# Two-layer decoder trunk: PSUM banks of the expert loop's side work from two pools, lo splits at the routing off GpSimd, and the second token norm split between ScalarE and VectorE

## Chip, cores and metric

The kernel runs on one core of a Trainium2 chip. The metric is the device time of one execution, the median of three runs. Below, PE is TensorE, DVE is VectorE, ACT is ScalarE, POOL is GpSimd and SP is SyncE, which issues the loads. PSUM is the memory that PE writes its sums to; a bank of it holds 128 x 512 floats.

## What is computed

A trunk of two layers over 256 tokens of width 1024, float32 throughout. The tokens are normed, and then each layer mixes tokens (three attention-like head groups from one input projection) and mixes channels: layer 0 with a dense SwiGLU, layer 1 with eight SwiGLU experts of which each token takes two.

```
x = layer_norm(x, ln_emb_g, ln_emb_b)
for l in range(DEPTH):
    mix = hybrid_mixer(x, w_in[l], ...)            # h = x @ w_in, three head groups, @ w_o
    x = layer_norm(DN_ALPHA * x + mix, ln1_g[l], ln1_b[l])
    f = swiglu(x, ...) if l % 2 == 0 else moe_swiglu(x, router, w_gate, w_up, w_down)
    x = layer_norm(DN_ALPHA * x + f, ln2_g[l], ln2_b[l])

def moe_swiglu(...):                               # D = 1024, 8 experts, inner width 3584
    logits = xt @ w_router
    top_v, top_i = lax.top_k(logits, 2)
    gates = sum(one_hot(top_i) * softmax(top_v))
    for e in range(8):
        y = y + gates[:, e:e+1] * swiglu(xt, w_gate[e], w_up[e], w_down[e])
```

## The kernel before

Every float32 operand of a product is split in two: a hi half, which is the value rounded for PE (`whi`, a cast on ACT, L151), and a lo half, what is left (`wlo`, a subtraction, L152, on DVE or, where a plan says so, on POOL). A product is then three matmuls: hi by hi, lo by hi, hi by lo (`mm3`, L161 to L163). Weights come in raw buffers by DMA; a raw buffer comes free when its lo half is done, and only then does SP load the next weights into it.

The order of the work on each engine is made by a scheduler from the order of the code, with ties written by hand: `after(i)` puts the next instructions behind instruction i, and `hold_splits(...)` is a plan for the next splits, each with what they stand behind and the engine of the lo half. `START` and `NEXT` are such plans for the first projection of layers 0 and 1 (True means POOL), and `R1`, `R2` say behind which split of the projection the two pieces of work on the second 128 tokens are recorded.

*Start.* The tokens come in two halves of 128. Each is normed (`stats`: mean and variance on DVE, the root on POOL; `norm`: L1247 and L1250, scalar_tensor_tensor on DVE, 512 columns at a time), transposed by PE (`pt`, L166) and split (`xhi`, `xlo`). Between them the input projection for the first half runs on PE (`pj`), over four weight splits of 832 columns and more.

*Routing.* After layer 1's norm DVE finds each token's two experts in small steps of 8 columns (L699 to L712), PE counts positions (`pc`), DVE compares them with a ramp (`pm`, L729, a 0/1 matrix per expert), and PE gathers the tokens of an expert by a matmul with it (`gx`, L741). ACT copies the hi halves (L751) and DVE the lo halves (L749) out of PSUM into `xg`. Meanwhile the first expert's weights are split; a plan in `gather` says how.

*Expert loop.* Eight experts of seven steps: gate and up sums (`eg`, two banks of the pool `wps`), SiLU on ACT (L919), a product on DVE (`hh`, L925), a transpose (`ht`) and the down sums (`y`, two banks of the pool `acc`). Each pool has four banks, given out in turn. From the second expert on each step has two forms, chosen at run time: heavy (three matmuls per product) if the expert has more than 64 tokens, light (two) if not. In this input experts 0, 3, 5 and 6 are heavy. Two experts make a pair. Side work of the pairs, called chores, is done one at a time at certain points of a step (`point`): the gather of the next pair (`gx`, then casts to `xg`), the transposed 0/1 matrices with the gates (`gsb`, L800 and L802, copied out by ACT at L805 and L806) and the scatter of an expert's result to its tokens (`sc`, L993 and L994, added to the sum on DVE, L999, `r`). A chore's bank comes free when its copy or addition is done, which `defer` puts four weight splits of 1024 columns later.

Of the kernel before, what the change touches and what calls it, by code (L numbers as in the profile page):

```python
# [10 lines left out]
F32 = mybir.dt.float32  # L11
F32R = mybir.dt.float32r
BF16 = mybir.dt.bfloat16
AF = mybir.ActivationFunctionType
ALU = mybir.AluOpType
# [3 lines left out]
P = 128  # L19
D = 1024  # L20
# [14 lines left out]
EARLY = 11  # L35
WT = (3, 4)
START = (False, True, False, True)
R1, R2 = (0, 1), (0, 5)
WF = 6
HBUF = 3  # L40
NEXT = (True, False, True, False)
R3 = (0, 7)
WS = (8,3)
FENT = ((0, None, 2), (1, None, SPL))
# [42 lines left out]
def trunk(ctx: ExitStack, tc: tile.TileContext, x, consts, mconsts, vecs, lnrows, w_in, w_uq, w_ukv, w_o,  # L87
          ffn_gu, ffn_dn, router, e_gate, e_up, e_down, out):
    nc = tc.nc
# [4 lines left out]
    acc = ctx.enter_context(tc.tile_pool(name="acc", bufs=4, space=PS))  # L94
    wps = ctx.enter_context(tc.tile_pool(name="wps", bufs=4, space=PS))

    def bank(pool, name):
        return pool.tile([P, 512], F32, tag="acc" if pool is acc else "wps", name=name)
# [37 lines left out]
    plan = []  # L136
    last = [None, None]

    def after(*ins):
        st = ExitStack()  # L140
        for i in ins:
            st.enter_context(tc.issue_after(i.ins))
        return st
# [2 lines left out]

    def split(src, n, lo_eng=None, to=None):
        hi, lo = to or [spl[0].tile([P, 1024], F32R, tag=t, name=t) for t in ("whi", "wlo")]
        ins, eng = plan.pop(0) if plan else ((), lo_eng)
        with after(*ins):  # L150
            last[0] = nc.scalar.copy(hi[:, :n], src)  # L151
            last[1] = (eng or nc.vector).tensor_tensor(lo[:, :n], src, hi.bitcast(F32)[:, :n], ALU.subtract)  # L152
        return hi, lo

    def hold_splits(*steps):
        plan.clear()
        for ins, eng, n in steps:
            plan.extend([(ins, eng)] * n)

    def mm3(o, ahi, alo, bhi, blo, start, stop):  # L160
        nc.tensor.matmul(o, ahi, bhi, start=start, stop=False)  # L161
# [475 lines left out]
    def moe(pool, raws2, raws3, r, gb, rw):  # L637
# [32 lines left out]
        for tt in range(2):  # L670
            x1 = ya[tt]
            pw, nm = ln_norm(*r[tt], gb, t0[:, tt], x1)
            lt = bank(acc, "lgp")
            for q in range(2):
# [5 lines left out]
                i1 = nc.scalar.copy(xt, pt)  # L680
# [44 lines left out]
        def gather(pr):  # L725
            pm = pool.tile([P, 2, 256], F32R, tag="pm", name="pm")
            for tt in range(2):
                for j in range(2):
                    ip = nc.vector.tensor_scalar(pm[:, tt, j * P:(j + 1) * P], iota, posm[:, tt, 2 * pr + j:2 * pr + j + 1],  # L729
                                            None, ALU.is_equal)  # L730
            if pr == 0:
                hold_splits(((), None, 2), ((pw,), nc.gpsimd, 2), ((i1, pw), nc.gpsimd, 1), ((i1, ip), None, 3))
            xgs = [pool.tile([P, KD, P, 2], F32R, tag="xg", name="xg", bufs=3) for j in range(2)]

            def half_part(k2, hl, n=0):
                src = (xth, xtl)[hl]
                b = bank(acc, "gx")
                for kk in range(2):
                    k = 2 * k2 + kk
                    for tt in range(2):  # L740
                        nc.tensor.matmul(b[:, kk * 256:(kk + 1) * 256], src[:, tt, k * P:(k + 1) * P], pm[:, tt, :],  # L741
                                         start=(kk == 0 and tt == 0), stop=(kk == 1 and tt == 1))

                def copies():
                    bv = b.rearrange("p (a b) -> p a b", b=256)
                    for j in range(2):
                        o = xgs[j][:, 2 * k2:2 * k2 + 2, :, hl]
                        if hl:
                            nc.vector.tensor_copy(o, bv[:, :, j * P:(j + 1) * P])  # L749
                        else:  # L750
                            nc.scalar.copy(o, bv[:, :, j * P:(j + 1) * P])  # L751

                defer(n, copies)

            def part(k2):
                for hl in range(2):
                    half_part(k2, hl)

            return pm, xgs, part, half_part
# [26 lines left out]
        def gather2(pr, pm):  # L786
            gs = pool.tile([P, 2], F32, tag="gs", name="gs")
            pT = pool.tile([P, 2, 2, P], F32R, tag="pTm", name="pTm")
            sc[pr] = [(gs[:, j:j + 1], pT[:, j]) for j in range(2)]

            for j in range(2):
                for tt in range(2):
                    nc.vector.tensor_scalar(pm[:, tt, j * P + 64:(j + 1) * P], iota[:, 64:P],
                                            posds[0][:, tt, 2 * pr + j:2 * pr + j + 1], None, ALU.is_equal)
            pmf = pm.bitcast(F32)

            def one(j):
                b = bank(acc, "gsb")
                for tt in range(2):
                    nc.tensor.matmul(b[:, 256:264], pmf[:, tt, j * P:(j + 1) * P], gates[:, tt, :], start=(tt == 0), stop=False)  # L800
                for tt in range(2):
                    nc.tensor.matmul(b[:, tt * P:(tt + 1) * P], pmf[:, tt, j * P:(j + 1) * P], ident, start=False, stop=(tt == 1))  # L802

                def copies():
                    nc.scalar.copy(gs[:, j:j + 1], b[:, 256 + 2 * pr + j:257 + 2 * pr + j])  # L805
                    nc.scalar.copy(pT[:, j, :, :], b[:, 0:256].rearrange("p (a b) -> p a b", b=P))  # L806

                defer(CHORE_N, copies)

            return one  # L810
# [9 lines left out]

        chores = []
        points = [0]

        def point():
            points[0] += 1
# [163 lines left out]
            nc.vector.scalar_tensor_tensor(y[1], yb[n], gs, y[0].bitcast(F32), ALU.mult, ALU.subtract)  # L989

        def scatter(n, tt, y, pT, last=False):
            b = bank(acc, "sc")
            nc.tensor.matmul(b, pT[:, tt, :], y[0], start=True, stop=False)  # L993
            nc.tensor.matmul(b, pT[:, tt, :], y[1], start=False, stop=True)  # L994
            if last:
                ln_sum(ya[tt], ya[tt], {n: b}, fsums[tt], 1.0, (n,))
            else:
                cs = slice(n * 512, (n + 1) * 512)
                defer(CHORE_N, lambda: nc.vector.tensor_tensor(ya[tt][:, cs], ya[tt][:, cs], b, ALU.add))  # L999
# [181 lines left out]
    with tc.tile_pool(name="spl", bufs=SPL, reuse_waits="tile") as spl[0], \  # L1181
# [35 lines left out]
        def start(mp):  # L1217
            z = mp.tile([P, 256], F32, tag="mk4", name="z")
            nc.gpsimd.memset(z, 0.0)
            keep_warm(bank(wps, "kw"), z, WS[0], z[:, 0:P])  # L1220
            xin = [cpool.tile([P, D], F32, tag="r", name="r", bufs=2) for _ in range(2)]
            load(xin[0], x[0:P, :])
            load(ident, mconsts[:, M_ID:M_ID + 128])
            t = gb_load(0)
            gb = [t[i // 2][:, (i % 2) * 512:(i % 2 + 1) * 512] for i in range(4)]
            load(xin[1], x[P:S, :])
            raw = win_a(0)
            load(vec, vecs)
            xhi, xlo = x3(F32R, "xhi"), x3(F32R, "xlo")
            xres = []  # L1230

            def stats(tt):
                st = small.tile([P, 2, 6], F32, tag="xst", name="xst", bufs=2)
                mv = small.tile([P, 4], F32, tag="xmv", name="xmv", bufs=2)
                for n in range(2):
                    nc.vector.bn_stats(st[:, n, :], xin[tt][:, n * 512:(n + 1) * 512])
                nc.vector.bn_aggr(mv[:, 0:2], st)
                nc.gpsimd.tensor_scalar_add(mv[:, 2:3], mv[:, 1:2], LN_EPS)
                rpow(mv[:, 3:4], mv[:, 2:3], 1)
                return mv  # L1240

            def norm(tt, mv):
                xr = pre.tile([P, D], F32, tag="xr%d" % tt, name="xr")
                xres.append(xr)
                for n in range(2):
                    cs = slice(n * 512, (n + 1) * 512)
                    nc.vector.scalar_tensor_tensor(xr[:, cs], xin[tt][:, cs], mv[:, 0:1], gb[n], ALU.subtract, ALU.mult)  # L1247
                for n in range(2):
                    cs = slice(n * 512, (n + 1) * 512)
                    i = nc.vector.scalar_tensor_tensor(xr[:, cs], xr[:, cs], mv[:, 3:4], gb[2 + n], ALU.mult, ALU.add)  # L1250
                return i

            def second(i):
                with after(last[1]):
                    norm(1, mv1)

            def third(i):
                with after(i):
                    pt = to_T(xres[1])
                split_T(pt, 1, xhi, xlo)  # L1260

            norm(0, stats(0))
            pts = to_T(xres[0])
            keep_warm(bank(wps, "kw"), z, WS[1], z[:, 0:P])
            mv1 = stats(1)
            split_T(pts, 0, xhi, xlo)
            rest = {R1: second, R2: third}
            hold_splits(*(((), nc.gpsimd if g else None, 1) for g in START))
            return raw, (xhi, xlo, xres), rest
# [141 lines left out]
```

## Time and profile before

| | |
|---|---|
| median of 3 runs | 1471.09 us (1469.09 to 1473.74) |
| the profiled execution | 1468.16 us |
| its span in the trace | 1466.0 us |
| around the span | 2.16 us |
| PE, DVE, ACT, POOL busy | 93%, 80%, 68%, 5% |
| mean granted PE clock | 0.987 of full |

The times of the profile are in microseconds from the span's start. The start lies at 0 to 31, the mixer and the dense channel mixer of layer 0 up to 338, the mixer of layer 1 up to 465, the routing at 465 to 488, the experts up to about 1450. Shares of busy time are means over these stages.

### The profile page before, as it was taken

The page shows a single profiled execution, that of the slowest core. Times are in us where ns is not written, and L with a number is a line of the kernel's source. Part 1 is how long each engine was busy: PE and PEld are TensorE (multiplying, and loading weights), DVE is VectorE, ACT ScalarE, POOL GpSimd, SP SyncE. Part 2 cuts the span into 40 slices and gives each one's busy share as a digit, 9 for nine tenths or more (in the row PEclk, how much of TensorE's full clock was granted, in tenths as well). Part 3 has the DMA queues.
Part 4 walks back from the last instruction along what each step waited for, and adds up shares of the span by engine and source line. Part 5 has one row for each costly group of instructions (what it writes and reads, how often), then busy time and mean ns, then how long its engine had stood idle before and what let it go on. Part 6 is the DMA issues. An engine that isn't in the chain of part 4 may idle for free. (4 is left out here: it accounts for less than half of the span.)

```text
span 1466.0 us, 18597 instructions
## 1 busy us (share of the span) xinstructions
PE 1359.3 (93%) x6927; PEld 1118.0 (76%) x6927; DVE 1176.5 (80%) x1256; ACT 997.0 (68%) x1073; POOL 78.4 (5%) x113
## 2 busy tenths in 40 slices
PE   7999999999999899988989999998999999999895
PEld 6987999998987688766666677866677787787663
DVE  6577655557677788899999987898998788788996
ACT  3564444444565677788978877787986777778794
POOL 3011000004102100000000000000000000000101
PEclk9999999999999999999999999999999999999998
DMA  6733555544534699999999998899998799899980
GB/s 264 276 135 115 189 186 186 188 157 153 194 116 201 231 339 356 375 365 349 420 406 369 419 382 323 325 367 348 407 419 342 295 357 357 311 358 389 357 363 30
DMA packets 63513, 429.46 MB, mean 293 GB/s; under 512 B 7058, under 2 KB 7570, under 8 KB 15268
## 3 DMA queue, kind: packets, MB, share of 16 engines
q1 hardware_dynamic: 63364, 427.81, 76.4%
q8 instruction: 81, 1.33, 0.4%
q14 instruction: 36, 0.29, 0.1%
q0 software_dynamic: 32, 0.03, 0.0%
HBM read 426.76 MB, written 1.05 MB: 292 GB/s over the span
## 5 line engine op out<-in xcount | busy, mean ns | idle before, releaser
L152 DVE TENSOR_TENSOR wlo<-raw,whi 128x2048 fp32r<-128x2048 f32 (+4 forms) x475 | 911.0, 1939 | 158.3 <-ACT whi L151 156.7
L151 ACT CAST whi<-raw 128x2048 fp32r<-128x2048 f32 (+4 forms) x482 | 771.0, 1619 | 250.5 <-PE gu L585 44.0
L898 PE MATMUL eg<-wlo,xg 128*128 128x512 f32 x448 | 185.6, 414 | 22.1 <-DVE wlo L152 19.0
L162 PE MATMUL eg<-wlo,xg 128*128 128x512 f32 x448 | 178.0, 397 | 0.8 <-DVE wlo L152 0.3
L161 PE MATMUL eg<-whi,xg 128*128 128x512 f32 x448 | 178.6, 399 | 0.0
L897 PE MATMUL eg<-whi,xg 128*128 128x512 f32 x448 | 178.4, 398 | 0.0
L163 PE MATMUL eg<-whi,xg 128*128 128x512 f32 x448 | 176.6, 394 | 0.0
L898 PEld LDWEIGHTS eg<-wlo,xg 128*128 128x128 f32 x448 | 84.4, 188 | 70.4 <-DVE wlo L152 54.9
L971 PE MATMUL y<-wlo,wk 128*128 128x512 f32 x224 | 94.2, 421 | 17.0 <-DVE wlo L152 15.8
L162 PEld LDWEIGHTS eg<-wlo,xg 128*128 128x128 f32 x448 | 86.9, 194 | 21.5 <-DVE wlo L152 5.4
L163 PEld LDWEIGHTS eg<-whi,xg 128*128 128x128 f32 x448 | 86.7, 194 | 17.3
L584 PE MATMUL gu<-xhi,whi 128*128 128x256 f32 x352 | 99.8, 283 | 0.1
L585 PE MATMUL gu<-xlo,whi 128*128 128x256 f32 x352 | 99.7, 283 | 0.2 <-DVE xlo L224 0.2
L161 PEld LDWEIGHTS eg<-whi,xg 128*128 128x128 f32 x448 | 86.9, 194 | 16.7
L586 PE MATMUL gu<-xhi,wlo 128*128 128x256 f32 x352 | 99.6, 283 | 0.0
L897 PEld LDWEIGHTS eg<-whi,xg 128*128 128x128 f32 x448 | 84.9, 189 | 15.0 <-ACT whi L151 0.5
L971 PE MATMUL y<-whi,wk 128*128 128x512 f32 x224 | 90.3, 403 | 3.6 <-DVE wk L945 1.5
L162 PE MATMUL y<-wlo,wk 128*128 128x512 f32 x224 | 88.0, 393 | 3.6 <-DVE wlo L152 3.4
L161 PE MATMUL y<-whi,wk 128*128 128x512 f32 x224 | 87.5, 392 | 0.4 <-ACT hh L919 0.4
L163 PE MATMUL y<-whi,wk 128*128 128x512 f32 x224 | 87.3, 390 | 0.0
L971 PEld LDWEIGHTS y<-wlo,wk 128*128 128x128 f32 x224 | 44.1, 197 | 42.7 <-DVE wlo L152 36.0
L584 PEld LDWEIGHTS gu<-xhi,whi 128*128 128x128 f32 x352 | 67.6, 192 | 0.7 <-DVE xlo L224 0.3
(313 smaller groups left out, 2111.8 us busy)
## 6 DMA issues: line engine op xcount, KB each, us to landing
raw<-in_e_gate SPq DMA_DIRECT2D x112, 1024.0 KB, 7.1
raw<-in_e_up SPq DMA_DIRECT2D x110, 1024.0 KB, 7.2
raw<-in_e_down SPq DMA_DIRECT2D x108, 1024.0 KB, 7.4
raw<-in_ffn_gu SPq DMA_DIRECT2D x22, 1024.0 KB, 4.8
raw<-in_ffn_dn SPq DMA_DIRECT2D x11, 1024.0 KB, 4.7
raw<-in_w_in SPq DMA_DIRECT2D x10, 960.0 KB, 4.7
raw<-in_w_o SPq DMA_DIRECT2D x8, 1024.0 KB, 6.7
gb<-in_lnrows SPq DMA_DIRECT2D x8, 512.0 KB, 5.3
```

Source lines behind the costliest of these rows:

```text
L151: last[0] = nc.scalar.copy(hi[:, :n], src)
L152: last[1] = (eng or nc.vector).tensor_tensor(lo[:, :n], src, hi.bitcast(F32)[:, :n], ALU.subtract)
L161: nc.tensor.matmul(o, ahi, bhi, start=start, stop=False)
L162: nc.tensor.matmul(o, ahi, blo, start=False, stop=False)
L163: return nc.tensor.matmul(o, alo, bhi, start=False, stop=stop)
L584: nc.tensor.matmul(o, hi[:, cs], xhi[:, k, :], start=(g == 0 and k == 0), stop=False)
L585: nc.tensor.matmul(o, hi[:, cs], xlo[:, k, :], start=False, stop=False)
L586: nc.tensor.matmul(o, lo[:, cs], xhi[:, k, :], start=False, stop=(g == 1 and k == 7))
L897: nc.tensor.matmul(bs[g], x2, sp[k // 4][0][:, cs], start=(k == 0), stop=False)
L898: nc.tensor.matmul(bs[g], x2, sp[k // 4][1][:, cs], start=False, stop=(k == 7))
L971: nc.tensor.matmul(yb[n], h2, sp[j // 2][i][:, j % 2 * D + n * 512:j % 2 * D + n * 512 + 512], start=(m == 0 and j == 0 and i == 0), stop= ...
```

## The change

It has four parts. The banks of chores come from a function that takes `acc` and `wps` by turns; the first pair's gather and the last scatters stay in `acc`. The plan at the routing gives all lo halves to DVE, and those of the third to fifth split stand behind the last `pm` (plans can hold an extra tie for the lo half). The second half of the tokens is normed by an activation on ACT (scale and bias from `stats`, the bias by one more POOL operation) and two tensor_tensor of 1024 columns on DVE, the second of them recorded later. And the first lo half of layer 1's projection goes from POOL to DVE.

```diff
-R1, R2 = (0, 1), (0, 5)
+R1, R2 = (0, 3), (0, 5)
-NEXT = (True, False, True, False)
+NEXT = (False, False, True, False)
...
-        ins, eng = plan.pop(0) if plan else ((), lo_eng)
+        ins, eng, late = plan.pop(0) if plan else ((), lo_eng, ())
         with after(*ins):
             last[0] = nc.scalar.copy(hi[:, :n], src)
+        with after(*ins, *late):
             last[1] = (eng or nc.vector).tensor_tensor(lo[:, :n], src, hi.bitcast(F32)[:, :n], ALU.subtract)
...
-                hold_splits(((), None, 2), ((pw,), nc.gpsimd, 2), ((i1, pw), nc.gpsimd, 1), ((i1, ip), None, 3))
+                hold_splits(((), None, 2), ((i1,), None, 3, ip), ((i1, ip), None, 3))
...
-                b = bank(acc, "gx")
+                b = bank(acc, "gx") if pr == 0 else step_bank("gx")
...
-                b = bank(acc, "gsb")
+                b = step_bank("gsb")
...
+        turns = [0]
+
+        def step_bank(name):
+            turns[0] += 1
+            return bank((acc, wps)[turns[0] % 2], name)
...
-            b = bank(acc, "sc")
+            b = bank(acc, "sc") if last else step_bank("sc")
...
             def second(i):
-                with after(last[1]):
-                    norm(1, mv1)
+                xr = pre.tile([P, D], F32, tag="xr1", name="xr")
+                xres.append(xr)
+                with after(last[0]):
+                    nc.scalar.activation(xr, xin[1], AF.Identity, bias=mv1[:, 2:3], scale=mv1[:, 3:4])
+                nc.vector.tensor_tensor(xr, xr, t[0], ALU.mult)
 
             def third(i):
+                nc.vector.tensor_tensor(xres[1], xres[1], t[1], ALU.add)
                 with after(i):
                     pt = to_T(xres[1])
                 split_T(pt, 1, xhi, xlo)
...
             mv1 = stats(1)
+            nc.gpsimd.tensor_scalar(mv1[:, 2:3], mv1[:, 0:1], mv1[:, 3:4], -1.0, ALU.mult, ALU.mult)
```

The change moves instructions in three places that matter below. In the start, the queue of DVE before the change holds (`xr` is the normed second half of the tokens, `gb` the scale and shift rows; a lo half of 832 belongs to one weight split):

```order
L152 TENSOR_TENSOR wlo<-raw,whi 128x832
L1247 SCALAR_TENSOR_TENSOR xr<-r,xmv,gb 128x512 x2
L1250 SCALAR_TENSOR_TENSOR xr<-xr,xmv,gb 128x512 x2
L152 TENSOR_TENSOR wlo<-raw,whi 128x832
L152 TENSOR_TENSOR wlo<-raw,whi 128x1024
```

and with the change, whose lines are numbered a little higher:

```order
L153 TENSOR_TENSOR wlo<-raw,whi 128x832
L1265 TENSOR_TENSOR xr<-xr,gb 128x1024
L153 TENSOR_TENSOR wlo<-raw,whi 128x832
L1268 TENSOR_TENSOR xr<-xr,gb 128x1024
L153 TENSOR_TENSOR wlo<-raw,whi 128x1024
```

Four operations on `xr` became two, and the lo half that stood behind all four now stands behind one. The other lo halves of 832 are POOL's in both. On ACT the new activation stands behind the second of four casts of 832, and on PE the transposes of `xr` come two matmuls later.

At the routing, DVE's queue before the change goes on like this from the 0/1 matrices (`cint`, `w`, `gates`, `gt` belong to the counts and gates):

```order
L729 TENSOR_SCALAR pm<-mc,posm 128x128 x4
L152 TENSOR_TENSOR wlo<-raw,whi 128x1024
L749 CAST xg<-gx 128x256 x2
L765 CAST cint<-cmax 128x1
L772 TENSOR_SCALAR w_5195<-ex 128x2
L773 RECIPROCAL w_5195<-w_5195 128x2
L749 CAST xg<-gx 128x256 x2
```

and with the change:

```order
L730 TENSOR_SCALAR pm<-mc,posm 128x128 x4
L153 TENSOR_TENSOR wlo<-raw,whi 128x1024
L750 CAST xg<-gx 128x256 x2
L153 TENSOR_TENSOR wlo<-raw,whi 128x1024
L750 CAST xg<-gx 128x256 x4
L153 TENSOR_TENSOR wlo<-raw,whi 128x1024 x2
L750 CAST xg<-gx 128x256 x2
L153 TENSOR_TENSOR wlo<-raw,whi 128x1024 x2
L766 CAST cint<-cmax 128x1
```

DVE has three lo halves more between the 0/1 matrices and the counts, where POOL has none left. The order of `gx` and `eg` on PE is the same in both.

In an odd expert's gather of the next pair, PE has before the change, between the gate sums and the up sums of one step:

```order
L166 MATMUL ht_9207<-mc_70,hh_8945 128x128 x4
L741 MATMUL gx_9272<-pm_9131,xth_4902 128x256 x4
L741 MATMUL gx_9336<-pm_9131,xtl_4903 128x256 x4
L741 MATMUL gx_9409<-pm_9131,xth_4902 128x256 x4
L856 COMPARE_AND_BRANCH
L161 MATMUL eg_9145<-whi_9216,xg_6510 128x512
L162 MATMUL eg_9145<-wlo_9217,xg_6510 128x512
```

and with the change, there and, behind the "...", after that step's up sums:

```order
L167 MATMUL ht_9207<-mc_70,hh_8945 128x128 x4
L742 MATMUL gx_9336<-pm_9131,xtl_4903 128x256 x4
L862 COMPARE_AND_BRANCH
L162 MATMUL eg_9145<-whi_9216,xg_6510 128x512
...
L742 MATMUL gx_9272<-pm_9131,xth_4902 128x256 x4
L862 COMPARE_AND_BRANCH
L162 MATMUL y_8882<-whi_9281,wk_5038 128x512
```

One of the three gather groups is left at its place; one stands behind the up sums, and the third (`gx_9409`) stands in the next step, ahead of its transpose.

## Rows read from the trace of the kernel before

**Rows 1.** The page, part 1: span, and busy time of each engine (instructions).
```profile
span 1466.0 us, 18597 instructions
...
PE 1359.3 (93%) x6927; PEld 1118.0 (76%) x6927; DVE 1176.5 (80%) x1256; ACT 997.0 (68%) x1073; POOL 78.4 (5%) x113
```
**Rows 2.** Timeline of PE in the start: start, duration, work [idle before, releaser].
```profile
21.91 0.72 PE L162 MATMUL pj<-wlo,xhi 128*128 128x416 f32 x1 [3.79 <-DVE wlo L152]
```
**Rows 3.** Timeline of DVE in the start.
```profile
14.75 4.84 DVE L1247 SCALAR_TENSOR_TENSOR xr<-r,xmv,gb 128x512 f32<-128x512 f32 x2
...
20.84 2.15 DVE L152 TENSOR_TENSOR wlo<-raw,whi 128x832 fp32r<-128x832 f32 x2
```
**Rows 4.** Timeline of POOL in the start.
```profile
14.64 4.40 POOL L152 TENSOR_TENSOR wlo<-raw,whi 128x832 fp32r<-128x832 f32 x2 [1.03 <-ACT whi L151]
```
**Rows 5.** Source line L1247: ns min/median/max, first and last start.
```profile
L1247 DVE SCALAR_TENSOR_TENSOR xr<-r,xmv,gb x4: 745/1602/2466, 8.5 to 17.1; 128x512 f32<-128x512 f32 x4
```
**Rows 6.** Timeline of POOL at the routing.
```profile
474.53 8.20 POOL L152 TENSOR_TENSOR wlo<-raw,whi 128x1024 fp32r<-128x1024 f32 x3 [5.08 <-ACT whi L151]
```
**Rows 7.** Timeline of DVE at the routing.
```profile
474.69 1.20 DVE L152 TENSOR_TENSOR wlo<-raw,whi 128x1024 fp32r<-128x1024 f32 x1
...
476.02 2.12 DVE L701 SCALAR_TENSOR_TENSOR eq<-lg,v,mc 128x8 f32<-128x8 f32 x1
...
478.37 2.08 DVE L707 TENSOR_SCALAR s<-eq,m 128x8 f32<-128x8 f32 x1
480.36 2.38 DVE L701 SCALAR_TENSOR_TENSOR eq<-lg,v,mc 128x8 f32<-128x8 f32 x1
...
483.11 0.22 DVE L701 SCALAR_TENSOR_TENSOR eq<-l,v,mc 128x8 f32<-128x8 f32 x1
```
**Rows 8.** Timeline of PE at the routing.
```profile
476.46 1.99 PE L207 MATMUL pc<-r,mc 128*128 128x256 f32 x8
483.84 0.17 PE L716 MATMUL pc<-sel,utb 128*128 128x8 bf16 x1 [5.39 <-DVE sel L711]
...
485.55 0.58 PE L741 MATMUL gx<-pm,xth 128*128 128x256 f32 x1 [0.78 <-DVE pm L729]
...
502.19 0.40 PE L161 MATMUL eg<-whi,xg 128*128 128x512 f32 x1
```
**Rows 9.** Groups of PE from 500 to 1450: busy, mean ns | idle before, releasers.
```profile
L741 PE MATMUL gx<-pm,xth 128*128 128x256 f32 x48 | 8.7, 302 | 8.0 <-DVE xg L749 5.6 <-DVE r L999 2.3
L741 PE MATMUL gx<-pm,xtl 128*128 128x256 f32 x48 | 8.2, 292 | 2.2 <-ACT xg L751 2.2
...
L800 PE MATMUL gsb<-gates,pm 128*128 128x8 f32 x32 | 4.4, 245 | 2.3 <-DVE r L999 2.3
```
**Rows 10.** Timeline of DVE in expert 1, a light one.
```profile
700.17 8.89 DVE L152 TENSOR_TENSOR wlo<-raw,whi 128x2048 fp32r<-128x2048 f32 x4
```
**Rows 11.** Window in a light expert: width, busy per engine, PE clock, DMA share, GB/s.
```profile
800.00:820.00 20.00, 18.97 (x76) 13.53 (x77) 20.00 (x12) 18.00 (x13) 0.00 (x0) 1.00 1.01 418
```
**Rows 12.** Timeline of ACT in the start.
```profile
12.89 3.25 ACT L151 CAST whi<-raw 128x832 fp32r<-128x832 f32 x4
```
**Rows 13.** Windows around idle stretches of PE (columns as in Rows 11).
```profile
18.00:22.00 4.00, 0.21 (x2) 0.09 (x1) 4.00 (x5) 0.88 (x1) 1.04 (x1) 0.92 1.00 421
...
486.00:488.00 2.00, 2.00 (x11) 2.00 (x11) 1.15 (x2) 0.68 (x2) 0.00 (x0) 0.50 0.53 221
488.00:490.00 2.00, 2.00 (x13) 1.85 (x12) 1.18 (x6) 0.67 (x2) 0.00 (x0) 0.74 0.87 283
...
1440.00:1444.00 4.00, 0.66 (x4) 0.42 (x4) 4.00 (x5) 0.98 (x2) 0.00 (x0) 1.00 0.01 2
```
**Rows 14.** Timeline of PE in a gather of expert 3.
```profile
893.93 0.73 PE L741 MATMUL gx<-pm,xtl 128*128 128x256 f32 x4 [0.75 <-ACT xg L751]
895.60 0.71 PE L741 MATMUL gx<-pm,xth 128*128 128x256 f32 x4 [0.94 <-DVE xg L749]
```
**Rows 15.** Timeline of DVE at the end of the dense channel mixer.
```profile
330.77 0.69 DVE L180 SCALAR_TENSOR_TENSOR r<-xr,fo 128x512 f32<-128x512 f32 x1 [2.80 <-PE fo L163]
```

More of the change, by code (lines that the diff above doesn't have):

```diff
@@ L156, in hold_splits @@
         plan.clear()
-        for ins, eng, n in steps:
-            plan.extend([(ins, eng)] * n)
+        for ins, eng, n, *late in steps:
+            plan.extend([(ins, eng, late)] * n)
     def mm3(o, ahi, alo, bhi, blo, start, stop):
```

## Prediction

> **What bounds the kernel now.** I read the page first: TensorE (PE) is busy for 93% of the span and VectorE (DVE) for 80% [rows 1]. That mean hides stages with different limits, so I went to the timelines of the stretches that the diff touches and asked which wait ends last.
>
> In the start PE waits: 3.79 us idle up to 21.91, released by a lo half from DVE [rows 2]. DVE was late because of two scalar_tensor_tensor of the token norm, 4.84 us together; the lo halves come two such operations later, at 20.84 [rows 3]. In the same time POOL (GpSimd) is at two lo halves of its own, 4.40 us from 14.64 [rows 4]. The same instruction on the first tokens takes 0.745 us at its shortest, and 2.466 at its longest [rows 5]. The two long ones end at 19.59, half a microsecond behind POOL's pair (19.04): of 4.84 us DVE worked some 0.75 twice and stood for the rest. I read that as mutual exclusion, in which POOL and DVE take turns, one whole instruction each.
>
> At the routing it is plainer. POOL makes three lo halves without a pause, 8.20 us from 474.53 [rows 6]. Three routing steps of 8 columns on DVE that meet them take 2.12, 2.08 and 2.38 us, and their like a moment later, with POOL empty, 0.22 [rows 7]. PE waits 5.39 us for that chain, and the gather matmuls begin at 485.55 [rows 8].
>
> In the expert loop PE stands 8.0 + 2.2 + 2.3 = 12.5 us at gather (gx) and gate-transpose (gsb) matmuls for a result that must leave a bank first [rows 9]. In heavy experts PE sets the pace, in light ones DVE: there four lo halves follow one another without a gap, 8.89 us [rows 10], and DMA is full at 418 GB/s [rows 11].
>
> **Start.** Removed from DVE are four scalar_tensor_tensor of 512 columns. Added are one POOL operation on a column (off the path, ahead of POOL's first lo half), one ScalarE activation over 1024 columns between the second and third hi half, and two plain tensor_tensor of 1024 on DVE. ScalarE's casts of 832 come 3.25 / 4 = 0.81 us apart [rows 12], so I estimate 1.0 for the activation: it ends near 15.6 (12.89 + 2 x 0.81 + 1.0), and the fourth hi half near 17.2. DVE's tensor_tensor of 1024 takes 1.20 [rows 7]. The product, ready at 15.6, meets POOL's first lo half, which runs from 14.64 to about 16.7. No row of before shows a plain tensor_tensor of DVE that starts under a running POOL instruction, so I bound it. Without exclusion the product ends at 16.8 and the third lo half at 17.9: PE resumes 4 us earlier. With the exclusion of [rows 3, 7] the product runs from 16.7 to 17.8; POOL's second lo half, ready since 17.2, has its turn to 19.7; the third lo half ends at 20.6, and PE resumes 1.3 us earlier. I take exclusion, since scalar_tensor_tensor also has two tensors in and is the nearest row.
>
> The Trainium skill (SBUF — State Buffer, "Who interferes with whom") says so of any VectorE instruction with two SBUF inputs against a GpSimd instruction that reads SBUF: the second to issue is blocked fully. By that rule product and sum stay exposed, and PE resumes 1.3 us earlier; without it 4.
>
> The clock adds to this. After 3.79 us of idle PE's granted clock fell from 2.4 to 1.2 GHz, mean 0.92 in 18 to 22; in 1440 to 1444, of which PE was idle for 3.3 us, it held at 1.00 [rows 13]. With 2.5 us of idle I expect no fall; that gives back about 1.2 us of the 13 matmuls and transposes that ran at half rate (0.16 each for the five of 416 columns, half of that for the eight transposes: 1.4 at most). Two matmuls of the fourth lo half now stand ahead of the transposes, and the sum is done at 21.8, about when PE gets there. Start: -2.5, bounds 0 and -4.
>
> **Routing.** Three lo halves leave POOL, so the three stalls go: 2.12 + 2.08 + 2.38 - 3 x 0.22 = 5.9 us. But PE has warm-up matmuls until 478.45 (476.46 + 1.99), and the chain is felt only from there: 483.84 - 478.5 = 5.3 us. Idle now comes in pieces under 1 us, so the clock, which was 0.50 in 486 to 488 and 0.74 in 488 to 490 [rows 13], should stay full: 2 x 0.50 + 2 x 0.26 = 1.5 us more. Against it: DVE gets three lo halves of 1.20 (3.6 us) among the gather's casts. They stand behind the four pm comparisons, so nothing of the routing is queued behind them; the casts of gx and the later lo halves are. From 480.5 DVE has six lo halves (7.2) and eight casts of a quarter of their size (0.3 to 0.4 each by that, some 3 in all), and is through near 491. PE, which was through with the gather and the first step's 48 gate and up matmuls at 502.2 [rows 8], gets there near 495.4 (5.3 and 1.5 earlier). PE stays the later one, and loses up to 0.8 us to a cast that comes late. The raw buffers of the three halves come free 1 to 3 us later than POOL freed them, later pairs earlier; SP, which waits for them to load again, is 0.8 us per load behind at the most. Routing: -6, bounds -4 and -7.
>
> **Banks in the expert loop.** In odd experts the three gather groups that stood behind one another are now split over both pools and over two places in the order. Two of four waits per odd expert go: 0.75 and 0.94 us idle, with the groups 1.67 apart where one lasts 0.73 [rows 14], so some 1.05 each with the refill, 2.1 together. Experts 3 and 5 are heavy, hence 4.2 us; in expert 1, light and paced by DVE, nothing. In even experts the first gsb still inherits the bank of the scatter just ahead of it, and gains nothing. What could be lost: in each odd expert two adds of scatters now stand together on DVE, and what waits for the second waits an add longer, some 0.6 us (512 columns, half of the 1.20 in [rows 7]). Banks: -4; bounds +1 (that add, 0.6 in expert 1, and a little in the even ones) and -9 (DVE's part of 12.5 in light experts set aside).
>
> **Layer 1's first lo half** moves from POOL to DVE into an idle stretch of 2.80 us [rows 15]. It takes about 1.0 (2.15 for one of 832 and one of 1024, [rows 3]): 0; without that cover 1.0.
>
> **Sum.** -2.5 - 6 - 4 = -12.5 us. The profiled execution took 1468.16 (span 1466.0 and 2.16 around it), 2.9 below the median of 1471.09. It would come to 1455.7; off the median 1458.6, so 1459. Its own range, not all terms at one end: 1454 to 1464.
>
> **Rivals.**
> - *Given back in the paced experts.* A light step loads six pieces of 128 x 2048 x 4 bytes, 6.29 MB, for which DMA needs 15.0 us at its 418 GB/s [rows 11], and DVE 6 x 2.22 = 13.3 and some small operations [rows 10]. Such steps live on what was loaded ahead. If the first expert's loads begin no earlier (the raw buffers above), the routing keeps 2 and the banks 1: -5.5, 1465.6. Against it: loads are released by DVE, which moves with PE. Chance 0.16.
> - *The change doesn't do what it says.* In each gather the wait that is left takes over what the others gave, and in the start the sum on DVE falls behind POOL's second lo half and the transposes wait for it. Only the routing is left: -6, 1465. For it: one engine answers both waits. Chance 0.10.
> - *More than said.* Start -4, routing -7, banks 7 of 12.5: -18, 1453. Chance 0.08.
> - *Slower.* The other pool holds the gate and up sums. A scatter, gather or gsb there keeps its bank until DVE or ScalarE drains it, and 30 now stand in that pool (half of 28 scatters, 24 gathers and 8 gsb). If a gate or up group inherits an undrained bank, PE pays what it pays today, up to 0.94 us. At 9 of 30 the 8.5 of start and routing are gone; at 15 it is 14.1 - 8.5 = +5.6, with nothing from the banks: 1476.7. Against it: in the new order well over a hundred instructions stand between a drain and the heir. Chance 0.08.
>
> **Numbers.** Forecast 0.58, rivals 0.16, 0.10, 0.08, 0.08. About 0.3% (4.4 us) is what a measurement of this kernel can tell from no change. Faster: 0.58 + 0.08 and 0.14 of the first two rivals, 0.80; within 0.3%: 0.12, the rest of them; slower: 0.08. The range of 1452 to 1468 takes in the forecast and the three faster rivals, and leaves out the slower one and the tails of the others.
>
> **What would show it.** In the start: PE resumes near 20.6 and keeps the full clock; DVE's product lasts over 2 us (exclusion) or 1.2 (none). At the routing: no such DVE step over 0.3 us, the first gather matmul near 480, clock 1.00 through 490, the first SiLU of the experts 6 us earlier. In the loop: PE's waits for gx and gsb down from 12.5 to some 7 us, the gather steps of heavy experts 1 to 2 us shorter, and no wait of an eg matmul for a bank. I am wrong if light experts show waits for DMA, if lo halves on DVE stall PE after 480, or if eg matmuls wait for DVE's r or xg.

## The result, and the profile after

The change made the kernel slower: 1482.66 us median of 6 runs (1477.59 to 1485.39) against 1470.43 of 6 (1466.88 to 1473.74), a ratio of 1.008, 95% interval 1.0055 to 1.0104. Forecast were 1459 us and a range of 1452 to 1468. The profiled execution took 1485.39 us, its span is 1483.5.

The start and the routing went as forecast. At the routing, the timeline of DVE, where [rows 7] had steps of over 2 us:

```profile
476.71 0.20 DVE L702 SCALAR_TENSOR_TENSOR eq<-lg,v,mc 128x8 f32<-128x8 f32 x1
...
477.53 0.22 DVE L708 TENSOR_SCALAR s<-eq,m 128x8 f32<-128x8 f32 x1
477.66 0.22 DVE L702 SCALAR_TENSOR_TENSOR eq<-lg,v,mc 128x8 f32<-128x8 f32 x1
```

and that of PE, against [rows 8]:

```profile
477.15 1.99 PE L208 MATMUL pc<-r,mc 128*128 128x256 f32 x8
478.99 0.17 PE L717 MATMUL pc<-sel,utb 128*128 128x8 bf16 x1
...
480.69 0.39 PE L742 MATMUL gx<-pm,xth 128*128 128x256 f32 x1 [0.78 <-DVE pm L730]
```

The three steps have 0.20 to 0.22 us, PE goes from its warm-up matmuls into `pc` without a gap (5.39 us before), and the gather begins 4.9 us earlier. The window that had a granted clock of 0.50 in [rows 13] has 1.00:

```profile
486.00:488.00 2.00, 2.00 (x14) 1.80 (x14) 1.91 (x3) 1.27 (x3) 0.00 (x0) 1.00 0.91 377
```

In the start, DVE, POOL and PE (three timelines; against [rows 2 to 4]):

```profile
16.41 2.03 DVE L1265 TENSOR_TENSOR xr<-xr,gb 128x1024 f32<-128x1024 f32 x1 [0.90 <-ACT xr L1264]
18.36 2.77 DVE L153 TENSOR_TENSOR wlo<-raw,whi 128x832 fp32r<-128x832 f32 x1
21.05 1.21 DVE L1268 TENSOR_TENSOR xr<-xr,gb 128x1024 f32<-128x1024 f32 x1
```

```profile
15.32 2.03 POOL L153 TENSOR_TENSOR wlo<-raw,whi 128x832 fp32r<-128x832 f32 x1 [0.86 <-ACT whi L151]
18.02 2.23 POOL L153 TENSOR_TENSOR wlo<-raw,whi 128x832 fp32r<-128x832 f32 x1 [0.67 <-ACT whi L151]
```

```profile
21.19 0.46 PE L163 MATMUL pj<-wlo,xhi 128*128 128x416 f32 x1 [2.37 <-DVE wlo L153]
```

The product lasts 2.03 us, not 1.2, and the lo half behind it 2.77, not 1.03: each stands until POOL's lo half is done, as forecast. PE waits 2.37 us instead of 3.79. It resumes at 21.19, 6.1 us after the tokens' first matmul (15.05), against 7.5 before (14.37 to 21.91).

The loss is in the expert loop. From the first SiLU of one expert to that of the next (the SiLU's starts in the trace), in us:

| expert | 0 | 1 | 2 | 3 | 4 | 5 | 6 |
|---|---|---|---|---|---|---|---|
| before | 117.7 | 114.7 | 111.8 | 129.1 | 114.0 | 131.1 | 125.3 |
| after | 117.7 | 122.8 | 112.4 | 135.9 | 113.8 | 138.1 | 125.7 |

The first SiLU comes 6.3 us earlier, at 491.8, and then the experts 1, 3 and 5, in which the next pair is gathered, lose 8.1, 6.8 and 7.0. The waits from 500 to the end of the span (who waited for whom: us, times, longest) answer to [rows 9]:

```profile
ACT xg L752 <- PE gx L742: 47.8, 12, 5.2
...
ACT gs L806 <- PE gsb L803: 13.7, 3, 5.7
PE y L163 <- DVE wlo L153: 12.9, 8, 1.8
...
PE gx L742 <- DVE xg L750: 2.8, 3, 0.9
PE gx L742 <- DVE r L1005: 2.3, 3, 0.8
PE gsb L801 <- DVE r L1005: 2.3, 3, 0.8
```

Before, the same view has:

```profile
ACT gs L805 <- PE gsb L802: 13.7, 3, 5.7
ACT xg L751 <- PE gx L741: 12.4, 3, 4.6
...
PE y L162 <- DVE wlo L152: 3.4, 4, 1.7
```

PE's waits at `gx` and `gsb` fell from 12.5 us to 7.4, as forecast. But ACT waits 47.8 us for gather groups, 12 times instead of 3, and PE waits 12.9 us instead of 3.4 for lo halves in the down sums of the heavy experts. How one leads to the other is seen in one gather of expert 3. ACT's timeline:

```profile
876.46 1.92 ACT L151 CAST whi<-raw 128x2048 fp32r<-128x2048 f32 x1
883.55 0.66 ACT L752 CAST xg<-gx 128x256 fp32r<-128x256 f32 x2 [5.18 <-PE gx L742]
884.09 1.91 ACT L151 CAST whi<-raw 128x2048 fp32r<-128x2048 f32 x1
```

then DVE's and PE's:

```profile
886.03 2.29 DVE L153 TENSOR_TENSOR wlo<-raw,whi 128x2048 fp32r<-128x2048 f32 x1 [2.79 <-ACT whi L151]
```

```profile
882.65 0.40 PE L164 MATMUL eg<-whi,xg 128*128 128x512 f32 x1
882.88 0.63 PE L742 MATMUL gx<-pm,xth 128*128 128x256 f32 x4
...
888.38 0.50 PE L163 MATMUL y<-wlo,wk 128*128 128x512 f32 x1 [1.83 <-DVE wlo L153]
```

ACT is through with its hi half at 878.4 and stands at the copy of a gather group that PE does only at 882.88, behind the last up sum. The next hi half, queued behind that copy, begins at 884.09. Its lo half begins at 886.03, after 2.79 us of idle on DVE, and PE, by then in the down sums, waits 1.83 us for it. Afterwards the granted clock falls:

```profile
888.00:890.00 2.00, 1.62 (x7) 1.36 (x8) 1.52 (x2) 1.85 (x2) 0.00 (x0) 0.97 0.41 74
890.00:892.00 2.00, 2.00 (x7) 1.52 (x6) 2.00 (x2) 0.82 (x1) 0.00 (x0) 0.50 0.89 369
```

Before, one of four hi copies per odd expert stood like that; now all four do. In the same gather of before (timeline of ACT) the one copy that waited, and one that didn't:

```profile
893.21 0.66 ACT L751 CAST xg<-gx 128x256 fp32r<-128x256 f32 x2 [4.60 <-PE gx L741]
...
898.31 0.70 ACT L751 CAST xg<-gx 128x256 fp32r<-128x256 f32 x2
```

The wait itself is the smaller part of the loss. From expert 1's first SiLU to the last SiLU, PE does the same 3265 matmuls (windows, before and after):

```profile
615.80:1435.82 820.02, 759.05 (x3265) 584.07 (x3264) 740.42 (x474) 650.57 (x536) 4.47 (x2) 1.00 0.93 363
609.50:1452.25 842.75, 772.11 (x3265) 591.83 (x3264) 741.48 (x474) 649.46 (x536) 4.47 (x2) 0.98 0.92 353
```

PE is idle for 9.7 us more, and for 13.1 us more it is busy with the same work. In windows of 2 us the granted clock falls once in this stretch before and eight times after, each time within some 1.5 us after a PE wait of 1.82 or 1.83 us for a lo half in the down sums. Before has two such waits, after eleven. (A fall can come without one: routing_alone, below, has four falls and two such waits.)

### The profile page after: what moved, and what is told of

It reads as the page before. It is cut to its first block, busy times and chain, and to the rows that moved or that the text cites. A ratio compares the mean times of both kernels' runs of the same rounds, so it can differ in the third digit from the quotient of the medians.

```text
span 1483.5 us, 18651 instructions
## 1 busy us (share of the span) xinstructions
PE 1373.3 (93%) x6927; PEld 1126.9 (76%) x6927; DVE 1174.8 (79%) x1258; ACT 996.9 (67%) x1074; POOL 68.2 (5%) x110
## 3 DMA queue, kind: packets, MB, share of 16 engines
HBM read 426.76 MB, written 1.05 MB: 288 GB/s over the span
## 5 line engine op out<-in xcount | busy, mean ns | idle before, releaser
L153 DVE TENSOR_TENSOR wlo<-raw,whi 128x2048 fp32r<-128x2048 f32 (+5 forms) x479 | 917.1, 1935 | 181.2 <-ACT whi L151 177.9
L977 PE MATMUL y<-wlo,wk 128*128 128x512 f32 x224 | 96.8, 432 | 20.7 <-DVE wlo L153 19.7
L163 PE MATMUL y<-wlo,wk 128*128 128x512 f32 x224 | 90.8, 405 | 12.9 <-DVE wlo L153 12.9
L977 PE MATMUL y<-whi,wk 128*128 128x512 f32 x224 | 92.3, 412 | 5.1 <-ACT whi L151 2.2
L162 PE MATMUL y<-whi,wk 128*128 128x512 f32 x224 | 89.9, 403 | 0.3 <-ACT hh L925 0.3
L164 PE MATMUL y<-whi,wk 128*128 128x512 f32 x224 | 89.7, 400 | 0.0
```

Source lines behind the costliest of these rows:

```text
L163: nc.tensor.matmul(o, ahi, blo, start=False, stop=False)
L164: return nc.tensor.matmul(o, alo, bhi, start=False, stop=stop)
L977: nc.tensor.matmul(yb[n], h2, sp[j // 2][i][:, j % 2 * D + n * 512:j % 2 * D + n * 512 + 512], start=(m == 0 and j == 0 and i == 0), stop= ...
```

## The experiments

Three theories stood to be told apart. **Q**: ACT takes its queue in order, and the copy of a hi group stands in it ahead of hi halves that PE needs sooner; the turns put the groups later on PE and left the copies where they were. **B**: the chores in the second pool hold banks that gate and up sums need. **F**: the faster front brings later stages out of step. Each run was compared with the kernel before on the same chip; that median was 1471.1 in the first four, 1471.1 in the next four and 1470.6 in the last.

**All banks from acc** (all_acc; start, routing and layer 1's lo half as changed).

```diff
-            return bank((acc, wps)[turns[0] % 2], name)
+            return bank(acc, name)
```

> The changed kernel with every chore's bank from acc again (start, routing and layer 1's lo half stay changed). Theory Q (queue): with the banks by turns, the gather's hi groups stand behind the up sums on PE, while ScalarE's copy of them stands where it stood; ScalarE waits, hi and lo halves come late. Then this kernel shows what the other parts give: 1470.4 - 8 = 1462, and ScalarE's wait for gx at 12 us as before. Theory B (banks: a chore in wps keeps a bank that a gate or up sum needs): the same, 1462. Theory F (the faster front brings DMA or light experts out of step, the banks are not to blame): 1478 or more.

Measured: 1462.15, ratio 0.9938 (0.9917 to 0.9959). The waits:

```profile
ACT xg L752 <- PE gx L742: 12.4, 3, 4.6
```

The other parts give 9 us; the front is not to blame, so F falls.

**Banks by turns alone** (banks_alone), in the kernel before (`step_bank` as in the change):

```diff
-                b = bank(acc, "gx")
+                b = bank(acc, "gx") if pr == 0 else step_bank("gx")
...
-                b = bank(acc, "gsb")
+                b = step_bank("gsb")
...
-            b = bank(acc, "sc")
+            b = bank(acc, "sc") if last else step_bank("sc")
```

> The kernel before with only the banks by turns. Theory Q and theory B: the odd experts 1, 3 and 5 lose some 7 us each, so 1470.4 + 21 = 1491, with ScalarE's wait for gx near 48 us. Theory F: about 1470.

Measured: 1491.23, ratio 1.0141 (1.0113 to 1.0169), 20 us slower, with

```profile
ACT xg L751 <- PE gx L741: 46.8, 12, 5.2
```

The loss is the banks', and the same with the old front.

**Gather from acc, scatter and gate-transpose by turns** (gx_acc).

```diff
-                b = bank(acc, "gx") if pr == 0 else step_bank("gx")
+                b = bank(acc, "gx")
```

> The changed kernel with the gather's banks from acc alone; scatters and gate-transposes keep the banks by turns. Theory Q: the gather is the cause, so 1462 to 1464. Theory B: 14 scatters and 4 gate-transposes still hold banks of wps, so at least a third of the 20 us stays: 1468 or more. Theory F: 1478 or more.

Measured: 1463.39, ratio 0.9953 (0.9938 to 0.9967). 18 chores still take banks of the second pool and cost nothing that can be told (1462.15 without). B in its general form falls.

**Copies tied later, banks by turns as changed** (tied6). Copies are put off by six units instead of four (a unit is a weight split of 1024 columns), and ACT's are tied behind the hi half recorded last. The edit moves ACT's copies of the gather, and DVE's by their putting off, but nothing in the place of `gx` on PE:

```diff
-HT_N, CHORE_N = 4, 4
+HT_N, CHORE_N, GX_N = 4, 4, 6
...
-                            nc.scalar.copy(o, bv[:, :, j * P:(j + 1) * P])
+                            with after(*([last[0]] if n else [])):
+                                nc.scalar.copy(o, bv[:, :, j * P:(j + 1) * P])
...
-                half[pr][3](0, 0, CHORE_N)
+                half[pr][3](0, 0, GX_N)
...
-            chores.extend((0, lambda i=i: half[pr][3](i // 2, i % 2, CHORE_N)) for i in range(1, 8))
+            chores.extend((0, lambda i=i: half[pr][3](i // 2, i % 2, GX_N)) for i in range(1, 8))
```

> The changed kernel, banks by turns and PE's order as they are, but the gather's copies are put off to six units instead of four, and ScalarE's are tied behind the hi half recorded last. Theory Q: ScalarE's wait for gx falls from 48 us to under 15, PE's waits for lo halves in the down sums (12.9 us) nearly go, and the time is 1462 to 1467. Theory B: banks are held a little longer, so the time stays at 1482 or grows. Theory F: 1482.

Measured: 1458.92, ratio 0.9924 (0.9897 to 0.9952): 24 us faster than the change with nothing but the copies' place altered. ACT no longer waits for gather groups at all (no such row is left), and the down sums' wait is 1.9 us. In the same gather of expert 3 the copy now stands behind four more hi halves, of which the last two are shown:

```profile
879.87 1.91 ACT L151 CAST whi<-raw 128x2048 fp32r<-128x2048 f32 x1 [1.21 <-PE y L163]
882.14 1.91 ACT L151 CAST whi<-raw 128x2048 fp32r<-128x2048 f32 x1 [0.36 <-PE y L164]
883.95 0.67 ACT L753 CAST xg<-gx 128x256 fp32r<-128x256 f32 x2
```

B said 1482 or more. Q is shown for the gather. What the tie does and what the later putting off does, no run takes apart.

**The turns begun at the other pool** (parity).

```diff
-            return bank((acc, wps)[turns[0] % 2], name)
+            return bank((wps, acc)[turns[0] % 2], name)
```

> The changed kernel with the turns begun at the other pool: now the lo groups of the gather, which VectorE copies out, take banks of wps and stand behind the up sums, and the hi groups stay in acc. Theory Q: the waiting moves with the bank to the engine that copies: VectorE's wait for gx grows from 16 us to 25 or more, ScalarE's falls from 48 to some 12; VectorE runs less far ahead of PE than ScalarE, so the stall is shorter: 1465 to 1475. Theory B: the same number of chores in wps, so 1482 as with the change.

Measured: 1488.19, ratio 1.0117 (1.0091 to 1.0143). Q's guess of where the waiting goes was wrong: it did not go to VectorE, and the time is above both expectations.

```profile
ACT xg L752 <- PE gx L742: 41.7, 9, 5.3
...
ACT gs L806 <- PE gsb L803: 27.4, 6, 5.7
...
DVE xg L750 <- PE gx L742: 9.6, 9, 2.0
...
ACT xg L752 <- PE sc L1000: 8.1, 3, 2.9
```

ACT waits 77 us, more than in any other run: in part for hi groups, which are in acc here, and now at six gate-transposes instead of three. So it isn't the pool of the hi groups that decides. With another sequence of turns, other chores are the late ones; what stays is that ACT pays for a late one. Why these come late was not followed up.

**All banks from acc, copies of the gather tied** (acc_tied6). The two edits of all_acc and tied6 together.

> The kernel with the gather's copies tied behind later hi halves, and all chores' banks from acc. Theory Q: ScalarE's 12 us of waits for gx go, but the copies now come out later, and with one pool PE waits longer for the bank of the group before: the idle of gx grows from 10 us to 15 or more. Between 1460 and 1468, so that the second pool is worth 2 us or more once the queue is mended. If the banks by turns bring nothing at all: 1459, like the run with both.

Measured: 1455.18, ratio 0.9884 (0.986 to 0.9909). Below both expectations. PE's waits for banks did not grow either:

```profile
PE gx L742 <- DVE xg L750: 5.1, 7, 0.9
...
PE gsb L802 <- DVE r L1006: 2.3, 3, 0.8
PE gx L742 <- DVE r L1006: 2.3, 3, 0.8
```

So the banks by turns, the part from which I forecast 4 us, bring no gain that can be told even with the queue mended: 1455.18 without them, 1458.92 with them (tied6).

**Gate-transposes' copies tied too, banks by turns** (tied_gsb6: tied6 and):

```diff
-                    nc.scalar.copy(gs[:, j:j + 1], b[:, 256 + 2 * pr + j:257 + 2 * pr + j])
-                    nc.scalar.copy(pT[:, j, :, :], b[:, 0:256].rearrange("p (a b) -> p a b", b=P))
-                defer(CHORE_N, copies)
+                    with after(last[0]):
+                        nc.scalar.copy(gs[:, j:j + 1], b[:, 256 + 2 * pr + j:257 + 2 * pr + j])
+                        nc.scalar.copy(pT[:, j, :, :], b[:, 0:256].rearrange("p (a b) -> p a b", b=P))
+                defer(6, copies)
```

> The run tied6 with the gate-transposes' copies put off and tied in the same way. Theory Q: the same queue stands still in the even experts 2, 4 and 6 (13.7 us of ScalarE's wait for gsb, three times); with the tie this goes, and the even experts become 0.5 to 2 us shorter each: 1455 to 1458. If that wait is hidden by what ScalarE has ahead: 1459.

Measured: 1449.70, ratio 0.9849 (0.9825 to 0.9872), more than expected; ACT's 13.7 us at `gs` are gone, and experts 2, 4 and 6 are 2.0, 1.8 and 1.9 us shorter than in tied6 (110.1, 111.7 and 123.8).

**Routing alone** (routing_alone): the changed plan in the kernel before.

> The kernel before with the lo halves at the routing on VectorE, nothing else. By the prediction: 1470.9 - 6 = 1465, the first SiLU of the experts 6 to 7 us earlier than the end of layer 1's norm would have it before. If the gain is given back in the paced experts: 1469.

Measured: 1464.17, ratio 0.9951 (0.9935 to 0.9967), 7.0 us faster; the median gives nothing back. (In its profiled execution experts 1 to 7 took 822.8 us against 820.0 before, with falls of the clock.)

**Both ties, all banks from acc** (acc_tied_all6).

> The run acc_tied6 (all banks from acc) with the gate-transposes' copies put off and tied too. Theory Q: the two mended queues add up: 1455.2 less the 5 to 6 us of the even experts, 1448 to 1451, and the second pool brings nothing at all once no copy stands ahead of its group. If the second pool does help with both ties: slower than the run tied_gsb6 (1449.7), at 1453.

Measured: 1448.44, ratio 0.9853 (0.9831 to 0.9875). Against tied_gsb6 at 1449.70 (runs of 1449.14 to 1453.01 there, 1445.42 to 1450.49 here) that is no difference that can be told. This beats both kernels, by 22 and 34 us.

**The same, copies put off by eight units instead of six** (acc_tied_all8).

> The same with copies put off by eight units instead of six. Theory Q: past the point at which ScalarE finds the group done, later is no better, and banks are held longer: the same as acc_tied_all6, or 1 to 5 us slower, with PE's idle at gx and gsb above its.

Measured: 1449.58, ratio 0.9862 (0.984 to 0.9884): the same. Eight units bring nothing over six.

**Start alone** (start_alone): the changed start in the kernel before.

> The kernel before with the start of the change, nothing else. By the prediction -2.5; by the changed kernel's trace, where layer 0's first residual operation came 2.1 us earlier, 1468.5 to 1469.5, which may not be told from no change. The trace decides: that operation near 136.6 instead of 138.8.

Measured: 1470.61 against 1470.56, ratio 0.9998 (0.9986 to 1.0011), no change. In its profiled execution the first residual operation of layer 0 stands at 136.49 instead of 138.76, as expected, and that of [rows 15] at 328.49, 2.3 us earlier. But there the tokens' first matmul had come 2.1 us earlier too (12.31 against 14.37), so only some 0.2 of the 2.3 us can be the change's. DVE's long pair shows here too, and the clock had fallen in the start:

```profile
15.10 1.71 DVE L1258 TENSOR_TENSOR xr<-xr,gb 128x1024 f32<-128x1024 f32 x1 [1.44 <-ACT xr L1257]
16.73 2.81 DVE L152 TENSOR_TENSOR wlo<-raw,whi 128x832 fp32r<-128x832 f32 x1
```

```profile
16.00:20.00 4.00, 2.63 (x7) 2.00 (x8) 4.00 (x3) 1.67 (x2) 1.96 (x1) 0.50 1.04 435
```

The added POOL operation, on one column, took 1.14 us here instead of 0.26 in the changed kernel's execution: it started at 12.65 beside a lo half of DVE that ran from 12.64 to 13.66, and ACT's activation waited 0.79 us for it. Of the eleven profiled executions with this start, all_acc and parity have the 1.14 too.

**No POOL in the start** (start_nopool: acc_tied_all6 and):

```diff
-START = (False, True, False, True)
+START = (False, False, False, False)
```

> The run acc_tied_all6 with all four lo halves of 832 in the start on VectorE. If product and POOL's lo halves exclude each other (2.03 and 2.77 us in the changed kernel for what takes 1.2 and 1.03), then without POOL there VectorE's operations have their own lengths, and though it has two lo halves more PE resumes near 19 instead of 21.2, and layer 0 begins 1 to 1.5 us earlier. If the long ones have another cause, VectorE is 2 us later instead.

Measured: 1447.90 against 1448.44, no difference that can be told. PE no longer waits in the start: the transposes of the second tokens begin 4.8 us after the tokens' first matmul (15.28 to 20.11), against 7.6 in acc_tied_all6 (14.26 to 21.82). Layer 0 was to begin 1 to 1.5 us earlier for it, and its first residual operation came later instead (134.60 against 133.05): at 110 to 120 the granted clock was 0.68 in this execution and 1.00 in the other. The timeline of DVE settles the question of the long operations:

```profile
14.72 1.96 DVE L153 TENSOR_TENSOR wlo<-raw,whi 128x832 fp32r<-128x832 f32 x2
16.65 1.22 DVE L1267 TENSOR_TENSOR xr<-xr,gb 128x1024 f32<-128x1024 f32 x1
17.79 1.02 DVE L153 TENSOR_TENSOR wlo<-raw,whi 128x832 fp32r<-128x832 f32 x1
```

Without POOL beside it the product takes 1.22 us and the lo half 1.02, where they took 2.03 and 2.77.

## Why the prediction was wrong, step by step

The terms, as forecast and as measured:

| term | forecast | measured |
|---|---|---|
| start | -2.5 | 0 alone (interval -2.1 to +1.6) |
| routing | -6 | -7.0 alone |
| start, routing and layer 1's lo half | -8.5 | -9.0 (all_acc) |
| banks | -4 | +20.5 (change less all_acc), +20.1 alone |

**The step that failed** is "Banks in the expert loop": "Two of four waits per odd expert go [...] so some 1.05 each with the refill, 2.1 together. Experts 3 and 5 are heavy, hence 4.2 us". I costed PE's side of the moved groups alone. The section on the change showed that a group now stands behind the up sums, and the profile of before had the price of that: ACT waited for a gather group 12.4 us in three waits, and for the second gate-transpose 13.7. The prediction does not mention them and never asks what is queued behind the copy on ACT: hi halves, from which DVE's lo halves and PE's next sums are made. Its sign for the loop came true (PE's waits down to 7.4 us) and the time still grew.

The runs put ACT's wait in its place. ACT's waits at `xg` and `gs`, PE's waits at `gx` and `gsb` (both summed over the rows of waits from 500 on), and the time from expert 1's first SiLU to the last SiLU:

| run | ACT at xg, gs | PE at gx, gsb | experts 1 to 7 |
|---|---|---|---|
| parity | 77.2 | 2.2 | 845.2 |
| after | 61.5 | 7.4 | 842.8 |
| banks_alone | 60.5 | 7.4 | 840.7 |
| before | 26.1 | 12.4 | 820.0 |
| all_acc | 26.1 | 12.4 | 822.0 |
| gx_acc | 26.1 | 12.4 | 820.2 |
| acc_tied6 | 13.7 | 9.7 | 814.0 |
| tied6 | 13.7 | 8.3 | 814.8 |
| tied_gsb6 | 0 | 8.3 | 809.2 |
| acc_tied_all6 | 0 | 9.7 | 807.9 |

Each row is one execution. The time follows ACT's wait in order, though not in proportion: 35.4 us more of it cost 22.8, the next 15.7 (parity) 2.4, and 26.1 less gave 12 to 14. Of the 22.8, PE's idle time makes 9.7 and its longer busy time, nearly all of it at the lower clock, 13.1. PE's own waits for banks, on which the term rested, go the other way if anywhere: where they are smallest the kernel is slowest. With ACT's queue mended the turns take 1.4 us of them away (tied6 against acc_tied6, tied_gsb6 against acc_tied_all6), and the time is no shorter.

**The rest of that part.** "In expert 1, light and paced by DVE, nothing": it lost most, 8.1 us: DVE, which paces it, waited 10.2 us for hi halves in it instead of 3.1. "In even experts nothing" held (0.6, -0.2 and 0.4 us). The bound of +1 was too near: it priced an addition on DVE, not a copy on ACT.

**The slower rival** had the right sign and the wrong mechanism. It priced a gate or up sum that inherits an undrained bank; no such wait is among the rows, and gx_acc, with 18 chores in the second pool, is not slower. That the gain is given back in the paced experts fell with all_acc and routing_alone.

**Routing.** Right in place and size. The chain was felt only from the end of the warm-up, DVE's lo halves behind `pm` stayed ahead of PE, and the clock held; 7.0 us alone against 6, within the bounds.

**Start.** Right in its mechanism: exclusion, a PE wait of 2.37 us where I had worked out 2.5, no fall of the clock in that execution (1.00 from 22 to 28). From the tokens' first matmul PE resumed 1.4 us earlier, where 1.3 were forecast. Small slips cancel in it (12.89 + 2 x 0.81 + 1.0 is 15.5, not 15.6; the activation took 1.24 us, not 1.0). The reading behind "no fall" was wrong, though, and that it held is luck: [rows 13] end with the wait in 1440 to 1444, and in the next window the clock is down (last section). As a term of the median it can't be shown: alone it measures as nothing within 2 us. In start_alone PE waited several times in the start and the clock was down at 16 to 20, so the 1.2 us that I had put on the clock are not had each time; and the POOL operation that I had put off the path was on it. Four runs with the same front (all_acc, gx_acc, tied6, acc_tied6) have the first SiLU at 491.14, 489.97, 493.55 and 490.59, so single executions differ by more than the term.

**Layer 1's lo half** cost nothing: it ran from 326.89 for 1.03 us, ahead of the residual operation at 328.64, as forecast.

Apart from the terms, the profiled execution of the change lost 2.8 us of its lead in layer 1's mixer (residual operation 2.1 us early at 328.64, the first one of layer 1's mixer 0.7 late at 459.50), where the clock fell (below). The executions of all_acc and tied6 show the same fall there (0.50 in 436 to 440 and in 440 to 444), those of acc_tied6 and start_nopool hold 1.00 throughout, with the same code in that place. It comes and goes with the execution; why is open.

## What to carry to other kernels

When an instruction moves later on one engine, look for its readers on the engines that take their queue in order: a copy that stays where it was now stands still there, and everything behind it with it. Read a wait on an engine that is "not the bottleneck" by what stands behind the waiting instruction; here 26 us of such waits on ScalarE, in the profile all along, were worth 12 to 14 us, while the 4 us forecast from the bound engine's own waits never showed. When that engine does run out of operands, count the clock as well as the wait: the clock was the larger part here. A tie that puts a copy behind work that is ready, with the copy put off by two units more, takes a few lines, and was worth more than any bank.

## What the runs showed of the hardware

A plain tensor_tensor of DVE with two operands in SBUF and one of POOL exclude each other for a whole instruction: 2.03 and 2.77 us beside POOL, 1.22 and 1.02 without. It holds the other way round too: POOL's operation on one column took 1.14 us beside a lo half of DVE and 0.26 without. By the Trainium skill (SBUF — State Buffer, "Who interferes with whom") the second to issue blocks fully; these numbers agree.

The granted clock of PE also fell where PE had been busy for the whole window before. In the changed kernel's execution, in layer 1's mixer:

```profile
434.00:436.00 2.00, 2.00 (x14) 1.69 (x13) 2.00 (x10) 0.34 (x2) 0.00 (x0) 0.98 0.63 266
436.00:438.00 2.00, 2.00 (x7) 1.59 (x8) 1.54 (x9) 0.19 (x1) 0.00 (x0) 0.50 0.00 0
```

It stayed at 1.2 GHz until about 443, and PE's lead over the execution of before went from 2.1 us at 340 to a lag of 0.5 at 442. In the execution of before it held at 2.4 GHz there. And in the expert loop a PE wait of 1.83 us was followed by the fall to 0.50 shown above. The longer one of before, 3.02 us in the window 1440 to 1444 of [rows 13], was followed by a fall as well, in the next window:

```profile
1444.00:1448.00 4.00, 2.84 (x7) 2.32 (x8) 0.78 (x2) 0.29 (x1) 0.00 (x0) 0.59 0.00 0
```

In the start of the changed kernel 2.37 us of idle were not followed by one. And of the eleven waits of 1.82 or 1.83 us in the changed kernel's loop three were not. So these rows give no length of a wait that the clock survives.
